# A feed-forward kernel on one Trainium2 core: down-weight blocks of 256 columns, and the sums of an up pair queued 12 ticks behind its request

## The chip, the cores and the metric

The kernel runs on one core of a Trainium2 chip. The metric is the device time of one execution in microseconds, as the median over runs. The engines are named as the profile names them: PE (TensorE, matmuls), DVE (VectorE), ACT (ScalarE), POOL (GpSimd) and SP (SyncE, which here issues the weight transfers). Each engine works through its own queue in the order in which the program wrote it.

## The reference, cut to what matters

The reference is one step of a two-layer hybrid backbone on 128 context tokens and 512 latent tokens, with a model width of 1024. Each layer ends in a gated feed-forward part, and the change lies in that part alone:

```
def conv_ffn(h, w_up, conv_w, conv_b, w_down):
    u = dwconv_centred(h @ w_up, conv_w, conv_b)
    val, g = jnp.split(u, 2, axis=-1)
    return (jax.nn.silu(g) * val) @ w_down
```

`w_up` is 1024 x 5632, `w_down` is 2816 x 1024, and the convolution has three taps along the tokens. The result, scaled by a gate, is added to the residual stream.

## The kernel before, in words

All products are made in float32 quality from float32r parts: a weight block is copied from HBM to a raw tile `wraw`, ACT rounds it to `whi` (L112), POOL subtracts to get `wlo` (L117), and each product takes three matmuls (`mm3`, L471 to L473). Tokens lie along the free axis: 644 columns (128 context, a gap of 4, 512 latent), taken in two halves of 322.

The 2816 hidden channels are 22 blocks of 128, in seven chunks of 3, 3, 3, 3, 3, 3 and 4 (`FF_CHUNKS`). The loop over chunks in `ffn` is

```
            for c, n in enumerate(FF_CHUNKS):
                ups(c, 0, early(c))
                if c:
                    down(c - 1)
                ups(c, early(c), n)
```

so that between two calls of `down` there are three up pairs. They are called A (the first after a down), B, and C (the one just ahead of the next down). An up pair (`up_pair`) makes value and gate of one hidden block from two up blocks of 128 columns by seven products of a Strassen-like scheme, in the order p1, p6, p5, p2, p7, p4, p3; each is 12 matmuls of 322 columns. Four of the seven use sums of the two weight blocks. `add_up` makes these on DVE (L139 to L142, tile `wsum`; L140 overwrites half of the second raw block in place), and `sum_part` splits them into `shi` (ACT) and `slo` (POOL for the first, DVE for the others, L119). Afterwards the pair's convolution (L1550 on ACT, then L317 on DVE, tile `ft`), the gate (L1566 on ACT, L1561 on DVE) and the split into `hidh` (ACT, L508) and `hidl` (DVE, L512) follow some ticks later.

`down` makes eight output tiles, 0 to 7; each is 18 matmuls (three hidden blocks, two halves, three terms) into one tile of PSUM named `wide`, which DVE adds to the residual `X` with two instructions (L317, 128x128 and 128x512). They are called X0 to X7. There are three `wide` buffers, used in turn by the down tiles and by the products (two products of a pair share one). So down tile n needs X(n-3) to be done; p1 and p6 of pair A need X5, p5 and p2 need X6, and p7 and p4 need X7.

The order of the work is written by a small planner. `tick` counts the program's position: one tick for three matmuls in a pair, two ticks for six matmuls in a down, so that a down tile has 6 ticks and a pair 28. `after(n, f)` writes f n ticks later. The class `Weights` holds the queue of weight blocks. `pump` requests the next block as long as a raw tile is free (`n_raw` = 3, used in turn); a raw tile comes free when its block has been split. `ahead` writes the splits of the next blocks, as far as there are free pairs of `whi`/`wlo` (`n_part` = 3, given back by `done`) and of `shi`/`slo` (`n_sum` = 4). For an up pair the order is add_up, split of the first block, two sums, split of the second block, the third sum. In `before` it writes `add_up` as soon as both blocks have been requested. `M.step` reads one block of the modulation maps with four matmuls and one DVE add; it runs beside the first feed-forward part until the maps are done, so the first four downs of layer 0 have it (their tiles are longer), and the last two of layer 0 and all six of layer 1 (called plain downs here) do not. The last chunk's down is another function (`last_down`) with blocks of 128 columns as before.

Of the kernel before, what the change touches and what calls it, by code (L numbers as in the profile page):

```python
# [9 lines left out]
F32 = mybir.dt.float32  # L10
# [11 lines left out]
NT = S0 + NS  # L22
NT2 = NT // 2
HALF = 322
OFF = 512 - HALF
# [8 lines left out]
HALVES = ((0, HALF), (HALF, NT))  # L34
# [5 lines left out]
FF_CHUNKS = (3, 3, 3, 3, 3, 3, 4)  # L40
# [2 lines left out]
N_STD = (2, 0, 3, 3)  # L43
N_WAIT = 1
AHEAD = 3
N_HID, N_FT = 4, 5
SUMS = (1, 8, 4)
FAST = (2, 2, 2, 2, 2, 1)
# [34 lines left out]
class Weights:  # L83
# [6 lines left out]
    def __init__(self, nc, pool, items):  # L90
        self.nc, self.pool, self.items = nc, pool, items
        self.loaded = self.freed = self.queued = self.next = 0
        self.raw, self.parts, self.pieces = {}, {}, []
        self.n_raw, self.n_part, self.n_sum = 3, 3, 4
        self.n_w = self.n_s = 0
        self.sums = self.over = None
        self.limit = len(items)

    def pump(self):
        while self.loaded < min(len(self.items), self.freed + self.n_raw, self.limit):  # L100
            ap, kt, w, _ = self.items[self.loaded]
            t = self.pool.tile([128, 8, 128], F32, name="wraw", tag="wraw", bufs=self.n_raw)[:, :kt, :w]
            self.nc.sync.dma_start(t, ap.rearrange("(k p) c -> p k c", p=128))
            self.raw[self.loaded] = t
            self.loaded += 1

    def split(self, pool, src, tag, bufs, low):
# [37 lines left out]
        self.parts.setdefault((i, "s"), []).append(  # L145
            self.split(self.sums, self.s[:, n], "s", self.n_sum, self.nc.vector if n else self.nc.gpsimd))

    def ahead(self, n=100):
        self.pump()
        for _ in range(n):  # L150
            if not self.pieces:
                i = self.queued
                if i == len(self.items):
                    return
                kind = self.items[i][3]
                if kind == "pair":
                    if not self.sums or self.loaded < i + 2:
                        return
                    self.pieces = [(0, lambda: self.add_up(i)), (1, lambda: self.block(i)),
                                   (2, lambda: self.sum_part(i, 0)), (2, lambda: self.sum_part(i, 1)),  # L160
                                   (1, lambda: self.block(i + 1)), (2, lambda: self.sum_part(i, 2))]
                    self.queued += 2
                else:
                    if self.loaded <= i or (kind == "held" and not self.over):
                        return
                    self.pieces = [(int(kind != "held"), lambda: self.block(i))]
                    self.queued += 1
            what, f = self.pieces[0]
            if (what == 1 and self.n_w == self.n_part) or (what == 2 and self.n_s == self.n_sum):
                return  # L170
            self.n_w += what == 1
            self.n_s += what == 2
            self.pieces.pop(0)
            f()
            self.pump()

    def upto(self, i):

        was = None
        while was != (self.queued, len(self.pieces)) and (self.queued <= i or self.pieces):  # L180
            was = self.queued, len(self.pieces)
            self.ahead(1)

    def get(self):
        for _ in range(8):
            if self.next not in self.parts:
                self.ahead(1)
        p = self.parts.pop(self.next)
        self.next += 1
        return p  # L190

    def get_pair(self):
        i = self.next
        while self.queued < i + 2 or (self.queued == i + 2 and self.pieces):
            self.ahead(1)
        return self.get(), self.get(), self.parts.pop((i, "s"))

    def done(self, w=1, s=0):
# [42 lines left out]
def tile_hybrid_step(ctx: ExitStack, tc: tile.TileContext, a, o):  # L241
# [121 lines left out]
    def add_w(ap, r0, kt, c0, w=128, kind=None):  # L363
        items.append((ap[r0:r0 + 128 * kt, c0:c0 + w], kt, w, kind))

    def held(n, n_std):
        return "held" if n >= n_std else None
# [32 lines left out]
    def ffn_items(l):  # L400
        up, dn = a["ffn_w_up"][l], a["ffn_w_down"][l]
        base = 0
        starts = []
        for n in FF_CHUNKS:
            starts.append(base)
            base += n

        def ups(c, j0, j1):
            for j in range(starts[c] + j0, starts[c] + j1):
                add_w(up, 0, 8, 128 * j, kind="pair" if j >= N_PLAIN else None)  # L410
                add_w(up, 0, 8, D_FF + 128 * j, kind="pair" if j >= N_PLAIN else None)

        def downs(c, last=False):
            for n in range(8):
                add_w(dn, 128 * starts[c], FF_CHUNKS[c], 128 * n, kind=held(n, N_STD[1 + 2 * l]) if last else None)
        for c, n in enumerate(FF_CHUNKS):
            ups(c, 0, early(c))
            if c:
                downs(c - 1)
            ups(c, early(c), n)  # L420
        downs(len(FF_CHUNKS) - 1, True)
        return starts
# [11 lines left out]


    k.bg, k.events, k.clock, k.count = [], [], 0, 0

    def after(n, f):
        heapq.heappush(k.events, (k.clock + n, k.count, f))
# [29 lines left out]
    def mm3(ps, w, x, c0, c1, p0, start, stop):  # L469
        (whi, wlo), (xhi, xlo) = w, x  # L470
        nc.tensor.matmul(ps[:whi.shape[-1], p0:p0 + c1 - c0], whi, xhi[:, c0:c1], start=start, stop=False)  # L471
        nc.tensor.matmul(ps[:whi.shape[-1], p0:p0 + c1 - c0], whi, xlo[:, c0:c1], start=False, stop=False)  # L472
        nc.tensor.matmul(ps[:whi.shape[-1], p0:p0 + c1 - c0], wlo, xhi[:, c0:c1], start=False, stop=stop)  # L473
# [6 lines left out]
    def wide():  # L480
        k.n_wide += 1
        return k.psum.tile([128, 1024], F32, name="wide", tag=k.wide_tag, bufs=k.wide_bufs)

    def gemm(xs, n=1, n_k=None, tail=True):

        n_k = n_k or len(xs)
        W.ahead()
        ws, ps = [], []
        for _ in range(n):
            ws.append(W.get())  # L490
            ps.append(wide())
        for kt, x in enumerate(xs):
            for w, p in zip(ws, ps):
                for c0, c1 in HALVES:
                    mm3(p, wk(w, kt), x, c0, c1, OFF + c0, kt == 0, kt == n_k - 1)
                tick(2)
        W.limit = len(items)
        W.done(n)
        M.step()
        if tail:  # L500
            W.ahead()
        return [p[:, OFF:OFF + NT] for p in ps]
# [995 lines left out]
    def ffn(l, final=None):  # L1498
        with ExitStack() as st:
# [124 lines left out]
            def down(c):  # L1624
                js = range(ffn_starts[c], ffn_starts[c] + FF_CHUNKS[c])
                until(lambda: all(j in hid for j in js))
                xs = [hid.pop(j) for j in js]
                for n in range(8):
                    ps = gemm(xs, 1, tail=False)[0]
                    for s, cols in STREAMS:  # L1630
                        fma(X[:, n, cols], ps[:, cols], modc[l][:, s, 40 + n:41 + n], X[:, n, cols])

# [349 lines left out]
```

## Time and profile before

| what | value |
|---|---|
| median of 3 runs | 2086.69 us (2076.94 to 2088.32) |
| profiled execution, its own time | 2080.74 us |
| its span on the core | 2078.7 us |
| mean granted TensorE clock | 0.962 of full speed |
| PE busy | 1880.9 us, 90% of the span |
| DVE busy | 1415.1 us, 68% |
| POOL busy | 1184.0 us, 57% |
| ACT busy | 964.7 us, 46% |

The profile is of a fourth execution, which took 2 us more than its span. Busy times are unions of instruction times on an engine; matmuls overlap each other at their ends, so PE can be busy without being at its peak. A row's releaser, shown as <-, is what ended the idle time before it.

### The profile page before, as it was taken

How to read it: one execution, taken by the hardware profiler on the slowest of the kernel's cores; microseconds unless marked ns; L12 is line 12 of the kernel's file. 1: busy time of each engine (PE TensorE's matmuls, PEld its weight loads, DVE VectorE, ACT ScalarE, POOL GpSimd, SP SyncE). 2: the span in 40 equal slices, each digit the busy share in tenths (PEclk: the TensorE clock that was granted, in tenths of full speed). 3: DMA queues.
4: the chain of work that ended last, by engine and by line, in shares of the span. 5: the costliest groups of instructions: out<-in, count | busy, mean ns of one | idle time of the engine just before them, and what ended most of it. 6: DMA issues, size and time to landing. Idle time of an engine off the chain costs nothing. (4 is left out here: it accounts for less than half of the span.)

```text
span 2078.7 us, 33613 instructions
## 1 busy us (share of the span) xinstructions
PE 1880.9 (90%) x12601; PEld 1719.6 (83%) x12601; DVE 1415.1 (68%) x2438; ACT 964.7 (46%) x1677; POOL 1184.0 (57%) x1528
## 2 busy tenths in 40 slices
PE   6878889999998999899999998988779899999997
PEld 4767668888887888798899997977679799999996
DVE  3477765655665337777778786676857778787874
ACT  3454453445444325433334344677725443443445
POOL 3235454333335445576557876478865577776772
PEclk9889999999999999999999999999889899999999
DMA  9554432112113342345542223112121122322221
GB/s 261 174 166 156 147 109 78 44 50 56 49 48 107 111 152 82 102 131 181 174 136 73 82 85 97 39 49 56 31 61 48 44 71 81 88 78 72 61 82 71
DMA packets 255577, 196.59 MB, mean 95 GB/s; under 512 B 13837, under 2 KB 233816, under 8 KB 255288
## 3 DMA queue, kind: packets, MB, share of 16 engines
q1 hardware_dynamic: 252664, 184.59, 29.6%
q0 software_dynamic: 2528, 7.13, 1.4%
q8 instruction: 99, 1.62, 0.3%
q10 hardware_dynamic: 224, 2.73, 0.3%
q14 instruction: 62, 0.51, 0.1%
HBM read 187.50 MB, written 6.92 MB: 94 GB/s over the span
## 5 line engine op out<-in xcount | busy, mean ns | idle before, releaser
L117 POOL TENSOR_TENSOR wlo<-wraw,whi 128x256 fp32r<-128x256 f32 (+1 forms) x835 | 710.7, 880 | 562.2 <-ACT whi L112 497.9
L471 PE MATMUL wide<-hhi,whi 128*128 128x322 f32 (+4 forms) x1072 | 358.7, 335 | 34.1 <-DVE X L317 15.2
L472 PE MATMUL wide<-hlo,whi 128*128 128x322 f32 (+4 forms) x1072 | 344.0, 321 | 7.5 <-DVE hlo L512 7.3
L473 PE MATMUL wide<-hhi,wlo 128*128 128x322 f32 (+4 forms) x1072 | 341.6, 319 | 0.0
L112 ACT CAST whi<-wraw 128x1024 fp32r<-128x1024 f32 (+1 forms) x259 | 217.4, 840 | 146.2 <-PE wide L473 71.1
L471 PEld LDWEIGHTS wide<-hhi,whi 128*128 128x128 f32 x1072 | 211.3, 197 | 52.9 <-ACT shi L112 15.4
L471 PE MATMUL gh<-hhi,whi 128*128 128x322 f32 (+3 forms) x688 | 232.1, 337 | 8.7 <-ACT zt L1178 8.7
L472 PEld LDWEIGHTS wide<-hlo,whi 128*128 128x128 f32 x1072 | 211.3, 197 | 12.2 <-DVE hlo L512 8.2
L472 PE MATMUL gh<-hlo,whi 128*128 128x322 f32 (+3 forms) x688 | 216.4, 315 | 1.3 <-DVE hlo L512 1.0
L473 PE MATMUL gh<-hhi,wlo 128*128 128x322 f32 (+3 forms) x688 | 215.9, 314 | 0.0
L473 PEld LDWEIGHTS wide<-hhi,wlo 128*128 128x128 f32 x1072 | 211.1, 197 | 0.0
L317 DVE SCALAR_TENSOR_TENSOR ft<-ft,PC 128x643 f32<-128x643 f32 x160 | 167.3, 1067 | 42.6 <-ACT ft L1550 40.6
L471 PE MATMUL wide<-hidh,whi 128*128 128x322 f32 (+2 forms) x600 | 191.3, 319 | 1.1 <-DVE ft L1608 1.1
L472 PE MATMUL wide<-hidl,whi 128*128 128x322 f32 (+2 forms) x600 | 187.0, 312 | 0.8 <-DVE hidl L512 0.8
L473 PE MATMUL wide<-hidh,wlo 128*128 128x322 f32 (+2 forms) x600 | 187.0, 312 | 0.0
L471 PEld LDWEIGHTS gh<-hhi,whi 128*128 128x128 f32 (+1 forms) x688 | 131.4, 191 | 33.7 <-issue 20.8
L317 DVE SCALAR_TENSOR_TENSOR X<-wide,modc,X 128x128 f32<-128x128 f32 (+3 forms) x276 | 128.0, 507 | 33.8 <-PE wide L473 33.8
L1550 ACT ACTIVATE ft<-ft,PC 128x644 f32<-128x644 f32 x80 | 73.9, 927 | 145.4 <-DVE ft L1615 135.3
L472 PEld LDWEIGHTS gh<-hlo,whi 128*128 128x128 f32 (+1 forms) x688 | 131.2, 191 | 2.4 <-DVE hlo L512 1.2
L473 PEld LDWEIGHTS gh<-hhi,wlo 128*128 128x128 f32 (+1 forms) x688 | 130.8, 190 | 0.6
L112 ACT CAST shi<-wsum 128x512 fp32r<-128x512 f32 x120 | 72.8, 617 | 123.8 <-DVE wsum L141 110.6
L471 PEld LDWEIGHTS wide<-hidh,whi 128*128 128x128 f32 x600 | 113.5, 189 | 14.5 <-issue 7.0
(379 smaller groups left out, 4606.6 us busy)
## 6 DMA issues: line engine op xcount, KB each, us to landing
wraw<-in_ffn_w_up_dram SPq DMA_DIRECT2D x88, 512.0 KB
mraw<-in_w_mod_dram SPq DMA_DIRECT2D x80, 512.0 KB
wraw<-in_ssd_attn_w_in_dram SPq DMA_DIRECT2D x42, 512.0 KB
wraw<-in_ffn_w_down_dram SPq DMA_DIRECT2D x96, 192.0 KB
E<-ad SPq DMA_DIRECT2D x16, 640.0 KB
mraw<-in_w_mod_dram SPq DMA_DIRECT2D x32, 256.0 KB
wraw<-in_ssd_attn_w_out_dram SPq DMA_DIRECT2D x16, 512.0 KB
wraw<-in_lru_w_in_dram SPq DMA_DIRECT2D x16, 512.0 KB
```

The costliest lines, as they stand in the source:

```text
L112: self.nc.scalar.copy(hi, src)
L117: low.tensor_sub(lo[:, q], src[:, q], hi[:, q].bitcast(F32))
L317: nc.vector.scalar_tensor_tensor(out, in0, scalar, in1, op0=op0, op1=op1, **kw)
L471: nc.tensor.matmul(ps[:whi.shape[-1], p0:p0 + c1 - c0], whi, xhi[:, c0:c1], start=start, stop=False)
L472: nc.tensor.matmul(ps[:whi.shape[-1], p0:p0 + c1 - c0], whi, xlo[:, c0:c1], start=False, stop=False)
L473: nc.tensor.matmul(ps[:whi.shape[-1], p0:p0 + c1 - c0], wlo, xhi[:, c0:c1], start=False, stop=stop)
L1550: after(at, lambda: nc.scalar.activation(out, u, AF.Identity, scale=par(cw, 2 * NF + t), bias=par(cb, t)))
```

## The change

A chunk's down weights are requested as four blocks of 256 columns in place of eight of 128 (384 KB each in place of 192 KB); `down` takes a block for two output tiles and gives it back after the second. The raw tile is the same 1024 columns, but laid out without gaps. The last chunk's down keeps its blocks. And `ahead` writes the sums of an up pair only when 12 ticks have passed since the request for its second block, unless the pair is needed at once (`get`, `get_pair` and `upto` pass `now=True`).

```
+LANDING = 12
...
     def pump(self):
         while self.loaded < min(len(self.items), self.freed + self.n_raw, self.limit):
             ap, kt, w, _ = self.items[self.loaded]
-            t = self.pool.tile([128, 8, 128], F32, name="wraw", tag="wraw", bufs=self.n_raw)[:, :kt, :w]
+            t = self.pool.tile([128, 1024], F32, name="wraw", tag="wraw", bufs=self.n_raw)[:, :kt * w].rearrange(
+                "p (k c) -> p k c", k=kt)
             self.nc.sync.dma_start(t, ap.rearrange("(k p) c -> p k c", p=128))
             self.raw[self.loaded] = t
+            self.asked[self.loaded] = self.clock()
...
-    def ahead(self, n=100):
+    def ahead(self, n=100, now=False):
...
                     if not self.sums or self.loaded < i + 2:
+                        return
+                    if not now and self.clock() < self.asked[i + 1] + LANDING:
                         return
...
         def downs(c, last=False):
+            if not last:
+                for n in range(4):
+                    add_w(dn, 128 * starts[c], FF_CHUNKS[c], 256 * n, 256)
+                return
             for n in range(8):
-                add_w(dn, 128 * starts[c], FF_CHUNKS[c], 128 * n, kind=held(n, N_STD[1 + 2 * l]) if last else None)
+                add_w(dn, 128 * starts[c], FF_CHUNKS[c], 128 * n, kind=held(n, N_STD[1 + 2 * l]))
...
                 for n in range(8):
-                    ps = gemm(xs, 1, tail=False)[0]
+                    W.ahead()
+                    if n % 2 == 0:
+                        whi, wlo = W.get()
+                    c = slice(128 * (n % 2), 128 * (n % 2) + 128)
+                    ps = wide()
+                    for kt, x in enumerate(xs):
+                        for c0, c1 in HALVES:
+                            mm3(ps, (whi[:, kt, c], wlo[:, kt, c]), x, c0, c1, OFF + c0, kt == 0, kt == len(xs) - 1)
+                        tick(2)
+                    W.done(n % 2)
+                    M.step()
+                    ps = ps[:, OFF:OFF + NT]
```

What this does to the queues is shown at three places of one plain down, the first of layer 1; the later ones have the same rows. On DVE, the rows around the sums of pair A before the change stand like this, beginning with X2 (two rows for each X):

```order
L317 SCALAR_TENSOR_TENSOR X<-wide,modc_113,X 128x128
L317 SCALAR_TENSOR_TENSOR X<-wide,modc_113,X 128x512
L1561 TENSOR_TENSOR ft<-ft 128x644
L512 TENSOR_TENSOR hidl<-ft,hidh 128x644
L317 SCALAR_TENSOR_TENSOR X<-wide,modc_113,X 128x128
L317 SCALAR_TENSOR_TENSOR X<-wide,modc_113,X 128x512
L317 SCALAR_TENSOR_TENSOR X<-wide,modc_113,X 128x128
L317 SCALAR_TENSOR_TENSOR X<-wide,modc_113,X 128x512
L139 TENSOR_TENSOR wsum<-wraw 128x512
L140 TENSOR_TENSOR wraw<-wraw 128x512
L141 TENSOR_TENSOR wsum<-wraw 128x512
L142 TENSOR_TENSOR wsum<-wraw,wsum 128x512
```

The same place on DVE after the change, beginning with X1 (lines are those of the changed kernel, where L143 to L146 are the sums, L1572 the gate's product, L523 `hidl`):

```order
L323 SCALAR_TENSOR_TENSOR X<-wide,modc_113,X 128x128
L323 SCALAR_TENSOR_TENSOR X<-wide,modc_113,X 128x512
L143 TENSOR_TENSOR wsum<-wraw 128x512
L144 TENSOR_TENSOR wraw<-wraw 128x512
L145 TENSOR_TENSOR wsum<-wraw 128x512
L146 TENSOR_TENSOR wsum<-wraw,wsum 128x512
L323 SCALAR_TENSOR_TENSOR X<-wide,modc_113,X 128x128
L323 SCALAR_TENSOR_TENSOR X<-wide,modc_113,X 128x512
L1572 TENSOR_TENSOR ft<-ft 128x644
L523 TENSOR_TENSOR hidl<-ft,hidh 128x644
L323 SCALAR_TENSOR_TENSOR X<-wide,modc_113,X 128x128
L323 SCALAR_TENSOR_TENSOR X<-wide,modc_113,X 128x512
```

The sums of pair A moved from behind X4 to behind X1, and with that ahead of X2, of the gate's product of pair C and of its `hidl`.

Further on in DVE's queue come the sums of pair B. Before the change the rows are these, from X6 on:

```order
L317 SCALAR_TENSOR_TENSOR X<-wide,modc_113,X 128x128
L317 SCALAR_TENSOR_TENSOR X<-wide,modc_113,X 128x512
L119 TENSOR_TENSOR slo<-wsum,shi 128x512
L139 TENSOR_TENSOR wsum<-wraw 128x512
L140 TENSOR_TENSOR wraw<-wraw 128x512
L141 TENSOR_TENSOR wsum<-wraw 128x512
L142 TENSOR_TENSOR wsum<-wraw,wsum 128x512
L317 SCALAR_TENSOR_TENSOR X<-wide,modc_113,X 128x128
L317 SCALAR_TENSOR_TENSOR X<-wide,modc_113,X 128x512
L119 TENSOR_TENSOR slo<-wsum,shi 128x512
L1603 TENSOR_TENSOR ft<-wide,ft 128x322
```

After the change they are these, from X5 on:

```order
L323 SCALAR_TENSOR_TENSOR X<-wide,modc_113,X 128x128
L323 SCALAR_TENSOR_TENSOR X<-wide,modc_113,X 128x512
L123 TENSOR_TENSOR slo<-wsum,shi 128x512
L143 TENSOR_TENSOR wsum<-wraw 128x512
L144 TENSOR_TENSOR wraw<-wraw 128x512
L145 TENSOR_TENSOR wsum<-wraw 128x512
L146 TENSOR_TENSOR wsum<-wraw,wsum 128x512
L323 SCALAR_TENSOR_TENSOR X<-wide,modc_113,X 128x128
L323 SCALAR_TENSOR_TENSOR X<-wide,modc_113,X 128x512
L323 SCALAR_TENSOR_TENSOR X<-wide,modc_113,X 128x128
L323 SCALAR_TENSOR_TENSOR X<-wide,modc_113,X 128x512
```

The sums of pair B stood between X6 and X7; now they stand ahead of both.

On ACT, the casts from the middle of the down to the first block of pair A (128x1024) stand like this before the change (`hidh` is L508, the gate's activation L1566):

```order
L112 CAST whi<-wraw 128x384 x2
L1566 ACTIVATE ft<-ft 128x644
L112 CAST whi<-wraw 128x384
L508 CAST hidh<-ft 128x644
L112 CAST whi<-wraw 128x384 x2
L112 CAST whi<-wraw 128x1024
L112 CAST shi<-wsum 128x512 x2
```

After the change they stand like this:

```order
L116 CAST whi<-wraw 128x768
L1577 ACTIVATE ft<-ft 128x644
L519 CAST hidh<-ft 128x644
L116 CAST whi<-wraw 128x1024
L116 CAST shi<-wsum 128x512 x2
L116 CAST whi<-wraw 128x1024
```

The down casts became fewer and larger, and the cast of pair A's first block moved up to stand right behind `hidh`; POOL's queue follows the same order with its `wlo` pieces.

## Rows read from the trace of the kernel before

**Rows 1.** The page: busy time, share of the span and instructions by engine.
```profile
PE 1880.9 (90%) x12601; PEld 1719.6 (83%) x12601; DVE 1415.1 (68%) x2438; ACT 964.7 (46%) x1677; POOL 1184.0 (57%) x1528
```

**Rows 2.** Windows: stretch, length, busy us (instructions) by engine, granted clock, DMA.
```profile
1733.00:1796.00 63.00, 60.86 (x399) 60.43 (x398) 49.79 (x68) 26.14 (x41) 45.99 (x55) 0.97 0.26 76
1796.00:1859.00 63.00, 59.67 (x399) 58.97 (x397) 50.20 (x68) 26.04 (x41) 46.39 (x55) 1.00 0.26 76
...
1922.00:1984.00 62.00, 60.25 (x394) 60.05 (x395) 49.26 (x67) 26.15 (x41) 46.41 (x55) 0.97 0.27 77
```

**Rows 3.** Waits of PE, 1640 to 2020: us in total, times, longest.
```profile
PE wide L471 <- DVE X L317: 13.9, 9, 2.1
```

**Rows 4.** Waits of PE, 860 to 1150, the downs with map steps.
```profile
PE wide L471 <- DVE X L317: 1.6, 3, 0.8
```

**Rows 5.** Waits of PE, 1150 to 1250, the plain downs of layer 0.
```profile
PE wide L471 <- DVE X L317: 5.0, 3, 2.1
```

**Rows 6.** Timeline of PE at three places: start, us, operation, [idle before <-releaser].
```profile
1735.60 0.39 PE L471 MATMUL wide<-hhi,whi 128*128 128x322 f32 x1 [2.14 <-DVE X L317]
1735.82 0.31 PE L472 MATMUL wide<-hlo,whi 128*128 128x322 f32 x1
1735.97 0.31 PE L473 MATMUL wide<-hhi,wlo 128*128 128x322 f32 x1
...
1798.51 0.39 PE L471 MATMUL wide<-hhi,whi 128*128 128x322 f32 x1 [2.15 <-DVE X L317]
...
1806.91 0.39 PE L471 MATMUL wide<-t3h,shi 128*128 128x322 f32 x1 [1.03 <-DVE X L317]
```

**Rows 7.** Timeline of DVE, one plain down and the start of pair A.
```profile
1717.13 3.72 DVE L317 SCALAR_TENSOR_TENSOR ft<-ft,PC 128x643 f32<-128x643 f32 x3
1720.77 1.91 DVE L317 SCALAR_TENSOR_TENSOR X<-wide,modc,X 128x128 f32<-128x128 f32 x4
...
1724.44 0.83 DVE L512 TENSOR_TENSOR hidl<-ft,hidh 128x644 fp32r<-128x644 f32 x1 [0.80 <-ACT hidh L508]
1725.19 1.92 DVE L317 SCALAR_TENSOR_TENSOR X<-wide,modc,X 128x128 f32<-128x128 f32 x4
1730.80 1.12 DVE L139 TENSOR_TENSOR wsum<-wraw 128x512 f32<-128x512 f32 x1 [3.69 <-DMA wraw<-in_ffn_w_up_dram]
...
1733.84 0.69 DVE L142 TENSOR_TENSOR wsum<-wraw,wsum 128x512 f32<-128x512 f32 x1
1734.45 1.00 DVE L317 SCALAR_TENSOR_TENSOR X<-wide,modc,X 128x128 f32<-128x128 f32 x2
...
1738.83 0.69 DVE L139 TENSOR_TENSOR wsum<-wraw 128x512 f32<-128x512 f32 x1 [0.50 <-DMA wraw<-in_ffn_w_up_dram]
...
1741.84 1.11 DVE L142 TENSOR_TENSOR wsum<-wraw,wsum 128x512 f32<-128x512 f32 x1
1742.88 1.00 DVE L317 SCALAR_TENSOR_TENSOR X<-wide,modc,X 128x128 f32<-128x128 f32 x2
```

**Rows 8.** Timeline of ACT, same stretch.
```profile
1710.03 0.51 ACT L112 CAST whi<-wraw 128x384 fp32r<-128x384 f32 x1
...
1723.68 0.73 ACT L508 CAST hidh<-ft 128x644 fp32r<-128x644 f32 x1 [1.59 <-DVE ft L1561]
...
1728.13 1.05 ACT L112 CAST whi<-wraw 128x1024 fp32r<-128x1024 f32 x1 [2.17 <-PE wide L473]
```

**Rows 9.** Timeline of POOL, same stretch; a 384-column block takes two pieces.
```profile
1713.72 1.16 POOL L117 TENSOR_TENSOR wlo<-wraw,whi 128x256 fp32r<-128x256 f32 x2
1714.85 0.76 POOL L1614 TENSOR_TENSOR ft<-ft,x 128x322 f32<-128x322 f32 x1
...
1729.26 3.27 POOL L117 TENSOR_TENSOR wlo<-wraw,whi 128x256 fp32r<-128x256 f32 x4 [1.85 <-ACT whi L112]
```

**Rows 10.** Timeline of SP's queue: requests for the second blocks of pairs A and B.
```profile
1726.32 0.37 SPq L103 DMA_DIRECT2D wraw<-in_ffn_w_up_dram  x1
...
1734.68 0.37 SPq L103 DMA_DIRECT2D wraw<-in_ffn_w_up_dram  x1
```

More of the change, by code (lines that the diff above doesn't have):

```diff
@@ L97, in __init__ @@
         self.limit = len(items)
+        self.clock, self.asked = (lambda: 0), {}
     def pump(self):
@@ L181, in upto @@
             was = self.queued, len(self.pieces)
-            self.ahead(1)
+            self.ahead(1, True)
     def get(self):
@@ L186, in get @@
             if self.next not in self.parts:
-                self.ahead(1)
+                self.ahead(1, True)
         p = self.parts.pop(self.next)
@@ L194, in get_pair @@
         while self.queued < i + 2 or (self.queued == i + 2 and self.pieces):
-            self.ahead(1)
+            self.ahead(1, True)
         return self.get(), self.get(), self.parts.pop((i, "s"))
@@ L436, in tile_hybrid_step @@
     k.bg, k.events, k.clock, k.count = [], [], 0, 0
+    W.clock = lambda: k.clock
     def after(n, f):
```

## The prediction

> **What bounds the kernel now.** I read the page first: PE is busy for 90% of the span, and no other engine is above 68% [rows 1]. Then the windows of one period (three pairs and a plain down) of layer 1: PE is busy 60 to 61 of 63 us, while DVE comes to 50 of 63 [rows 2]. So in the part that the change touches PE is the bound, and all that can be won is its idle time and its half-clock time; but DVE is near enough to full that a few microseconds of waiting in its queue reach PE.
>
> The waits of PE give the amount. Between 1640 and 2020 PE waits 13.9 us in nine waits for DVE's X [rows 3]; in the two plain downs of layer 0 it is 5.0 us in three [rows 5]; in the downs with map steps only 1.6 us [rows 4]. Together that is 20.5 us. The clock adds to it: in two of the three windows shown the granted clock is 0.97, a loss of some 0.03 x 63 = 1.9 us each [rows 2].
>
> The timelines say why. At 1735.60 the first matmul of pair A has waited 2.14 us for X, at 1798.51 another 2.15 us; there, at 1806.91, p7 (the operand t3h) waits 1.03 us more [rows 6]. DVE had X3 and X4 done by 1727.1 and then stood idle 3.69 us in the sums of pair A, whose second block was still in flight. The sums took 1730.80 to 1734.5, X5 came only after them, and PE went on [rows 7]. The request for that block is at 1726.32, so it took 4.5 us to the first sum [rows 10, 7]. The sums of pair B stand ahead of X7 in the same way: they begin at 1738.83 and X7 at 1742.88 [rows 7].
>
> **A clock for one down.** Matmuls start 0.15 us apart (1735.82, 1735.97 [rows 6]). A tile of 18 takes 2.7 us, a product of 12 takes 1.8. The eight tiles end at 1735.60 - 2.14 = 1733.5, so tile 0 starts at 1711.9 and tile n ends at 1711.9 + 2.7(n+1). With no wait p5 would start at 1733.5 + 3.6 = 1737.1 and p7 at 1740.7. Before, p7 starts 1806.91 - 1798.51 + 2.15 = 10.55 us after the end of tile 7, which is 1744.0 on this clock. In the period shown the half clock ate the second wait instead, and p7 starts at about 1735.6 + 7.2 + 1.6 = 1744.4. I take 1744.2 for before, a loss of 3.5 us per plain down.
>
> **The change, part by part.** *Fewer, larger blocks.* ACT casts 384 columns in 0.51 and 1024 in 1.05 [rows 8], so 768 is about 0.83: four of those are 3.3 us per down, where eight small ones were 4.1. POOL takes 1.16 us for a block's two pieces and 3.27 for four full ones [rows 9]: three full ones are 2.45, four blocks 9.8 us, where eight were 9.3. SP issues four requests for eight. None of this is on PE's path by its sum, since ACT and POOL are idle 37 and 17 us of such a window [rows 2]. But the first blocks sit in POOL's queue ahead of pair C's last additions: the block of 1713.72 stands just ahead of L1614 [rows 9], and its split grows by 1.3 us. What is late next is C's convolution on ACT and DVE. Of the conv rows on DVE (three in 3.72 us from 1717.13 [rows 7]) the last two wait for it. X1, done at 1721.7 before, comes at 1721.7 to 1722.3.
>
> *An earlier request for pair A.* Three blocks of the down are split by the time tile 0 starts, so A's second block is asked for when that POOL split ends: 1713.72 + 2.45 plus up to 0.8 of delay, about 1716.2 to 1717. With 4.5 us it lands by 1721.5. The idle 3.69 us of DVE is gone: this part does what it says.
>
> *But the sums now stand behind X1.* They start at 1721.7 to 1722.3 and take 3.1 us (POOL idle) to 3.7 (as from 1730.80 to 1734.5 [rows 7]). X2 ends 0.93 later, at 1725.7 to 1726.9, while tile 5 is due at 1725.4: PE waits 0.4 to 1.5 us. X3 comes after the gate's product and `hidl`, some 3.2 us after X2, against a tile 6 then due 2.7 later: another 0.5 to 0.8.
>
> *The sums of pair B are the new place.* They need B's second block, which goes into the raw tile of A's first block and so waits for POOL's split of that. The chain, from X2 on: the gate's product 0.83, `hidh` on ACT 0.73, A's first cast right behind it 1.05, four POOL pieces 3.27 [rows 8, 9], then the request. From X2's end at 1725.7 that makes 1731.8, and with a later X2 and slower pieces 1733. A request takes 1738.83 - 1734.68 = 4.15 us to the first sum [rows 10, 7], so the sums of B start at 1735.9 to 1737.1. They take 3.7 to 4.1 (POOL is at work then), and X6, which stands behind them now, ends 0.95 later: 1740.6 to 1742. p5 was due at 1737.1 plus the 1 to 2 us just lost. It starts at 1740.8 to 1742; p7, 3.6 later, at 1744.4 to 1745.6, and X7 is then long done. Against 1744.2 before, that is +0.2 to +1.4 us per plain down. I take +0.8, the middle, because the two ends differ only by whether DVE and POOL get in each other's way, and both kinds of rows stand in this stretch. So the 12 ticks do not cover it: they are two tiles, 5.4 us, from the writing of A's first split, but that split runs far behind its place in the program.
>
> At one place a page speaks against the change. The last of the four sums takes 0.69 us at 1733.84 and 1.11 at 1741.84, where POOL is at work [rows 7]; I priced the sums of B between these. The Trainium skill (SBUF — State Buffer, Who interferes with whom) says that a DVE instruction with two SBUF inputs and a GpSimd instruction that reads SBUF block each other fully, not in part. By that rule four sums could each wait out a POOL piece.
>
> **The sum.** Eight plain downs (six in layer 1, two in layer 0) x 0.8 = +6.4 us, bounds +1.6 to +11.2. The four downs with map steps have tiles longer by four matmuls and a DVE add; there the chain has about 5 us more room before p5, so I count their 1.6 us as won, bounds 0 to -1.6. The half clock: before, one that follows the first wait is hidden by the second; after, one that follows the wait of p5 is not, and costs its 1.6 us; one that follows the wait of tile 5 is. I take it in one down out of six or so, +2 us, bounds 0 and 8 x 1.6 = +13. Together +6.4 - 1.6 + 2 = +7 us. The profiled execution took 2080.74 us, which makes about 2088; it is 6 us below the median of the runs shown, and from that median, 2086.7, I come to 2094.
>
> **The rivals.** *The stall vanishes (faster).* If B's second block lands before DVE reaches the sums of B, X6 follows at once. DVE is there after X5 and one `slo`, at about 1734; p5 stays unstalled if X6 is done by about 1738.5, so the sums must start by 1733.8, 2.1 us earlier than my best chain. It needs A's first cast to run about 2 us earlier, as if it didn't sit behind `hidh`. Then a plain down loses only the 1 to 2 us at tiles 5 and 6: a gain of 8 x 2 + 1.6 = 18 us, or 2069. For it: DVE's 3.69 us of idle do go. Against it: the rows on ACT and POOL in the order of the change.
>
> *The change does nothing in sum.* The losses of tiles 5, 6 and p5 just replace those of p1 and p7: 2087 with a few us either way. It is the low end of my chain.
>
> *The clock falls at every new wait.* The wait of p5 is 2 to 3 us, as long as the ones of 2.14 to 2.15 of which some are followed by a half clock. If all are: 6.4 + 13 - 1.6 = +18, 2105.
>
> *DVE is blocked a whole POOL piece per sum.* A piece is 3.27 / 4 = 0.82, so each sum would take up to 0.69 + 0.82 = 1.51 and the four of B 6.0 in place of 4: 8 x 2 = +16 more, about 2110. The row of 1.11 speaks against it, and it is the rule of the Trainium skill (SBUF — State Buffer) at its strictest.
>
> **How the numbers follow.** My forecast has 0.5; the stall vanishing 0.17; nothing in sum 0.15; the clock 0.13; the blocked sums 0.05. A measurement of this kernel tells about 0.5%, 10 us, from no change. The first rival is faster by that. Forecast cases up to +10 us are the same, and I put 0.3 of its 0.5 there, with 0.14 from nothing in sum and 0.02 from a weak form of the clock; the rest, 0.37, is slower. The range goes from 2078 (below "nothing in sum" and short of a full gain) to 2108 (the clock case), and leaves out most of the first rival and the blocked sums.
>
> **What would show it.** Right: on DVE no long wait for a DMA ahead of pair A's sums; waits of PE for X at tiles 5 and 6 (on `hidh`) of 0.4 to 1.5 us, none at p1, and one of 2 to 4 us at p5 (operand `hhi`, block `whi`); the request for B's second block at 1731.8 to 1733 on this clock, with DVE waiting for it. Wrong: p5 without a wait and PE's waits for X in 1640 to 2020 well under 14 us; or new waits in the pairs, from late `slo`, which I priced at nothing because those sums are written earlier than before.

## The result: 1.6% slower

The changed kernel takes 2116.38 us (median of 4 runs, 2113.11 to 2117.38) where the kernel before takes 2086.02 (also of 4): a ratio on record of 1.0161, 95% interval [1.0138, 1.0185]. The plain quotient of the two medians is 1.0146 and lies in that interval. The prediction had 2094 us and a range up to 2108. So the direction was the one forecast, and the size was about four times the forecast +7 us. To a slowdown clear of the noise it had given 0.37, less than to no change.

The page of the changed kernel gives the busy times. PE is busy 14 us longer than in [rows 1], the span is 32.4 us longer (2078.7 to 2111.1), and the mean granted clock is 0.959 in place of 0.962.

```profile
span 2111.1 us, 33257 instructions
...
PE 1895.1 (90%) x12601; PEld 1726.4 (82%) x12601; DVE 1410.7 (67%) x2438; ACT 955.1 (45%) x1629; POOL 1154.4 (55%) x1480
```

Where the 32.4 us are can be read from marks that both timelines have: in each feed-forward part the one matmul of the first pair that waits 3.9 to 4.1 us for DVE (`hhi,shi`), and the first matmul of its `last_down`. In layer 0 they stand at 848.88 and 1267.28 before and at 847.23 and 1286.97 after: 418.4 us have become 439.7. In layer 1 they stand at 1633.51 and 2026.86, and at 1652.62 and 2060.80: 393.4 have become 408.2. That is +21.3 and +14.8; all the rest of the kernel together is 3.8 us shorter.

### The profile page after: what moved, and what is told of

The parts are those of the page before. It is cut to its first block, busy times and chain, and to the rows that moved or that the text cites. A ratio compares the mean times of both kernels' runs of the same rounds, so it can differ in the third digit from the quotient of the medians.

```text
span 2111.1 us, 33257 instructions
## 1 busy us (share of the span) xinstructions
PE 1895.1 (90%) x12601; PEld 1726.4 (82%) x12601; DVE 1410.7 (67%) x2438; ACT 955.1 (45%) x1629; POOL 1154.4 (55%) x1480
## 5 line engine op out<-in xcount | busy, mean ns | idle before, releaser
L121 POOL TENSOR_TENSOR wlo<-wraw,whi 128x256 fp32r<-128x256 f32 x787 | 672.3, 884 | 653.2 <-ACT whi L116 572.3
L116 ACT CAST whi<-wraw 128x1024 fp32r<-128x1024 f32 (+2 forms) x211 | 208.4, 989 | 151.8 <-PE wide L484 74.4
L323 DVE SCALAR_TENSOR_TENSOR ft<-ft,PC 128x643 f32<-128x643 f32 x160 | 175.2, 1109 | 46.8 <-ACT ft L1561 44.8
L483 PEld LDWEIGHTS wide<-hidl,whi 128*128 128x128 f32 x600 | 115.4, 192 | 1.0 <-DVE hidl L523 1.0
```

Of the source, the lines that this page charges most:

```text
L116: self.nc.scalar.copy(hi, src)
L121: low.tensor_sub(lo[:, q], src[:, q], hi[:, q].bitcast(F32))
L323: nc.vector.scalar_tensor_tensor(out, in0, scalar, in1, op0=op0, op1=op1, **kw)
```

## The profile after

**A plain down.** This is DVE's timeline of one, in layer 1 (start, duration, instruction, in brackets the idle time ahead of it and what ended it), from X1 to X6 and X7; it answers to [rows 7].

```profile
1740.48 1.00 DVE L323 SCALAR_TENSOR_TENSOR X<-wide,modc,X 128x128 f32<-128x128 f32 x2
1741.40 0.99 DVE L143 TENSOR_TENSOR wsum<-wraw 128x512 f32<-128x512 f32 x1
...
1743.88 0.69 DVE L146 TENSOR_TENSOR wsum<-wraw,wsum 128x512 f32<-128x512 f32 x1
1744.49 1.00 DVE L323 SCALAR_TENSOR_TENSOR X<-wide,modc,X 128x128 f32<-128x128 f32 x2
...
1755.52 0.99 DVE L143 TENSOR_TENSOR wsum<-wraw 128x512 f32<-128x512 f32 x1 [2.93 <-DMA wraw<-in_ffn_w_up_dram]
...
1758.84 1.10 DVE L146 TENSOR_TENSOR wsum<-wraw,wsum 128x512 f32<-128x512 f32 x1
1759.87 1.91 DVE L323 SCALAR_TENSOR_TENSOR X<-wide,modc,X 128x128 f32<-128x128 f32 x4
```

The sums of A start right behind X1, with no wait for a transfer; X2 stands behind them. The sums of B wait 2.93 us for their second block, and X6 stands behind those. On SP's queue these are the requests for the second blocks of A and B. The one of B came 5.9 us after X2's end (1745.49), and the sums 4.15 us after it.

```profile
1736.00 0.37 SPq L106 DMA_DIRECT2D wraw<-in_ffn_w_up_dram  x1
...
1751.37 0.37 SPq L106 DMA_DIRECT2D wraw<-in_ffn_w_up_dram  x1
```

On PE's timeline of the same down the first row here is the start of tile 0; then come the rows with a wait for X: the first matmuls of tiles 5 and 6 and of p5, and, further down, of p5 behind the next down. Behind the first p5 the matmuls of 0.31 us become ones of 0.47, for 3.2 us. The granted clock of that stretch (1762.6 to 1765.8) is 0.50, the lower of its two levels (1.2 in place of 2.4 GHz); this is what half clock means here, and nothing hides it at this place.

```profile
1730.59 0.41 PE L482 MATMUL wide<-hidh,whi 128*128 128x322 f32 x1
...
1745.63 0.39 PE L482 MATMUL wide<-hidh,whi 128*128 128x322 f32 x1 [1.10 <-DVE X L323]
...
1748.92 0.39 PE L482 MATMUL wide<-hidh,whi 128*128 128x322 f32 x1 [0.39 <-DVE X L323]
...
1761.01 0.39 PE L482 MATMUL wide<-hhi,whi 128*128 128x322 f32 x1 [2.93 <-DVE X L323]
...
1762.59 0.47 PE L483 MATMUL wide<-hlo,whi 128*128 128x322 f32 x1
...
1827.39 0.61 PE L482 MATMUL wide<-hhi,whi 128*128 128x322 f32 x1 [2.93 <-DVE X L323]
```

The down of 1745.63 and the four behind it (1812.01, 1878.39, 1943.26, 2007.41) are 66.4, 66.4, 64.9 and 64.2 us apart, 65.4 in the mean. Before, p1 of 1672.83 and of 1986.43 are five periods apart, 62.7 us each. The windows of two of the periods show the clock that separates those of 66.4 us from those of 64.2 and 64.9: 0.97 and 1.00 (columns as in [rows 2]).

```profile
1761.00:1827.00 66.00, 61.69 (x396) 60.32 (x396) 48.91 (x67) 25.39 (x37) 43.78 (x52) 0.97 0.24 72
...
1894.00:1958.00 64.00, 59.95 (x397) 58.63 (x396) 48.45 (x67) 25.40 (x37) 43.30 (x50) 1.00 0.25 75
```

**A down with map steps.** The waits of PE between 860 and 1150 are no longer those of [rows 4]. None is for X; `M.step` waits for its map block, 9.8 us in four times, and twice for DVE, 2.3 us.

```profile
PE mt L338 <- DMA mraw<-in_w_mod_dram: 9.8, 4, 3.7
PE mt L338 <- DVE wsum L143: 2.3, 2, 1.6
```

The longest of them is the second of these rows of PE, and the next fence has SP's queue ahead of it. Between the map request of 926.92 and that of 938.58 stand the two requests of an up pair, and both have to wait until a raw tile is free. The block that PE waits for at 944.77 is the one of 938.58. There are two map tiles in turn, and PE had read the one that this block goes into by 934.74 (the row of 934.10). So the request came 3.8 us late, and PE's wait is 3.7.

```profile
934.10 0.64 PE L338 MATMUL mt<-mraw,scp 128*32 128x256 f32 x8
...
944.77 1.08 PE L338 MATMUL mt<-mraw,scp 128*32 128x256 f32 x8 [3.71 <-DMA mraw<-in_w_mod_dram]
```

```profile
926.92 0.44 SPq L229 DMA_DIRECT2D mraw<-in_w_mod_dram  x1
935.34 3.15 SPq L106 DMA_DIRECT2D wraw<-in_ffn_w_up_dram  x2
938.58 7.65 SPq L229 DMA_DIRECT2D mraw<-in_w_mod_dram  x3
```

In the kernel before, SP's queue in the same stretch has a map request behind each small down block or two.

```profile
926.55 0.45 SPq L223 DMA_DIRECT2D mraw<-in_w_mod_dram  x1
933.01 3.41 SPq L103 DMA_DIRECT2D wraw<-in_ffn_w_down_dram  x2
936.51 2.20 SPq L223 DMA_DIRECT2D mraw<-in_w_mod_dram  x2
939.46 0.38 SPq L103 DMA_DIRECT2D wraw<-in_ffn_w_down_dram  x1
942.10 0.33 SPq L223 DMA_DIRECT2D mraw<-in_w_mod_dram  x1
943.29 0.38 SPq L103 DMA_DIRECT2D wraw<-in_ffn_w_down_dram  x1
945.56 0.33 SPq L223 DMA_DIRECT2D mraw<-in_w_mod_dram  x1
```

So the theory after the result has two separate parts. In the plain downs X6 stands behind sums of B whose block is in flight. In the downs with map steps the map requests stand on SP's queue behind requests that wait for a raw tile. Its rivals: the larger blocks are slow in themselves (POOL, DMA engines, raw tiles); or a wait removed anywhere comes back elsewhere.

The gate, the second half of the change, does nothing here. With blocks of 256 columns a gate of 0 ticks and one of 12 give the same program, instruction for instruction and wait for wait, on all five engines: the splits of the down blocks already hold the sums back to the same ticks. Whatever the changed kernel loses is the blocks' doing, with the order that they bring.

## The experiments

The kernel before ran beside each on the same chip (medians of 2078 to 2081 us there), so ratios to it are compared. "Map waits" are PE's waits for `mraw` in 860 to 1150; "layer 0" and "layer 1" are the lengths between the marks above. These three columns are in us and come from the one profiled execution of each kernel, the ratio from all of its executions.

| kernel | ratio to before, 95% | layer 0 | layer 1 | map waits |
|---|---|---|---|---|
| before | 1 | 418.4 | 393.4 | 0 |
| after | 1.0161 [1.0138, 1.0185] | 439.7 | 408.2 | 9.8 |
| e3_maps_on_act | 1.0099 [1.0080, 1.0118] | 424.3 | 406.5 | 0.7 |
| e5_plain_only | 1.0113 [1.0096, 1.0131] | 428.1 | 404.9 | 0 |
| e4_landing24 | 1.0096 [1.0073, 1.0119] | 440.4 | 391.5 | 14.5 |
| e13_landing13 | 1.0004 [0.9988, 1.0019] | 430.5 | 385.4 | 11.3 |
| e7_both_undone | 0.9978 [0.9965, 0.9991] | 423.0 | 391.3 | 4.3 |

### The maps, in two ways

e3_maps_on_act asks for the map blocks from ACT's queue during the first feed-forward part:

```
-            self.nc.sync.dma_start(t, ap)
+            self.queue.dma_start(t, ap)
...
+    M.queue = nc.scalar
     ffn(0)
```

> The changed kernel, but during the first feed-forward part the blocks of the modulation maps are requested from ACT's queue and no longer from SP's. Theory (in the downs with map steps the map requests stand on SP's queue behind both requests of an up pair, the second of which waits for a raw tile): the waits of PE for mraw and for the DVE add of the map block (9.8 and 2.3 us in 860 to 1150) and their half clock go, 12 to 16 us: 2100 to 2104 us, ratio 1.006 to 1.009; layer 1 stays as in the changed kernel (20.7 us of waits for X). Rival (larger blocks take the DMA engines or raw tiles from the maps, whatever queue asks for them): the waits for mraw stay, 2113 to 2117 us, ratio 1.013 to 1.016.

e5_plain_only keeps blocks of 128 columns in the four downs that have map steps:

```
+NARROW = 4
...
-            if not last:
+            if not last and (l or c >= NARROW):
```

> The changed kernel, but the first four downs of layer 0, those with map steps, keep eight blocks of 128 columns. Theory (the loss has two separate parts): layer 0's waits for mraw go, and the plain downs keep their waits at tile 5, 6 and p5, so about 16 us less than the changed kernel, 2098 to 2104 us, ratio 1.005 to 1.009; this sizes the two parts. Rival (the loss of layer 0 comes from the gate in the plan and not from the blocks): the time stays at 2112 to 2117 us.

Both are faster than the changed kernel, where the rivals had next to no gain, but both gained less than forecast: the ratios are 0.001 and 0.002 above the theory's ranges. Layer 0 gets 15.4 us back by the one and 11.7 by the other. In layer 1, where neither edit changes anything, it is 1.7 and 3.3, so by some 3 us such a length differs between executions. In e3 the blocks are as large as in the changed kernel, and yet the map waits are gone: it was the place in SP's queue, not the transfers. The Trainium skill (DMA: Bandwidth & Descriptors, Rules for kernel authors) says that spreading DMAs over the issuing engines brings no bandwidth and only saves issue time. Here it brings 0.6%, because a request no longer stands behind one that waits.

The control for it is the same edit on the kernel before, in which PE waited for 1.3 us in all ahead of a map step.

> The kernel before with one edit, the maps requested from ACT's queue during the first feed-forward part. Theory (only the changed order of requests on SP made the maps late; in the kernel before they wait 1.4 us at most in SP's queue and cost PE 1.3 us): no difference, ratio 0.997 to 1.002. Rival (the other queue is worth something by itself, and the gain of e3_maps_on_act and e8_wide_a12_maps is partly that): ratio 0.995 or less.

e12_before_maps has the ratio 1.0033 [1.0021, 1.0045], a little slower than expected: PE's waits for X in 860 to 1150 go from 1.6 [rows 4] to 6.4 us. So the other queue is worth nothing by itself. ACT's waits and its timeline show what it costs:

```profile
ACT whi L112 <- PE mt L333: 70.6, 30, 5.2
```

```profile
1029.67 0.34 ACTq L224 DMA_DIRECT2D mraw<-in_w_mod_dram  x1
1030.13 1.05 ACT L112 CAST whi<-wraw 128x1024 fp32r<-128x1024 f32 x1 [2.94 <-PE mt L333]
```

Now the casts of the weight blocks stand on ACT's queue behind map requests, and these wait until PE has read a map tile. Before, no cast waits for `mt`. In the third of the four downs the request for B's second block comes 26.6 us after the down's first matmul, where it came after 25.7, and PE waits 2.2 us for X at p7 in place of 0.3. A request that waits holds up what stands behind it here too, only on another queue. The links between the cast and X were not followed one by one.

### The place of the sums, with blocks of 256 columns

e4_landing24 changes one number, `LANDING = 24`: A's sums go behind X3, B's behind X7, C's behind the last combination of pair A.

> The changed kernel with a gate of 24 ticks in place of 12. In the program pair A's sums then stand behind X3 and pair B's behind X7. Theory (in plain downs the order of the sums against the X is what costs, not the size of the blocks): PE's waits at tiles 5 and 6 and at p5 go in all eight plain downs, and with them the waits of before at p1; the map waits of layer 0 stay. 2078 to 2086 us, ratio 0.995 to 1.000. Rival (the larger blocks themselves make casts and POOL pieces late, or later sums make shi and slo late in the pairs): waits for shi or slo of 2 us or more per down take their place, 2105 us or more, ratio 1.009 or more.

It had the ratio 1.0096, which by its number alone is the rival's. The traces say otherwise: layer 1 takes 391.5 us in place of 408.2, less than before, with no wait of the sums for a transfer, and all that is lost is in layer 0, where the map waits have grown to 14.5 us. The theory's range was missed by two things: those 4.7 us more, and a wait of 2.0 us per plain down that is left at tile 7, for the X4 that stands behind the sums of A.

e13_landing13 is the closest cut: `LANDING = 13`. In all twelve downs one tick more moves the sums of B from ahead of X6 to behind it (in those with map steps also behind the map block's add), and that is all: the queues of the other four engines are the same, instruction for instruction.

> The changed kernel with a gate of 13 ticks in place of 12, one number. In the program only the sums of pair B move in the plain downs, from ahead of X6 to behind it; those of A stay behind X1, and C's ahead of pair A's last combination. Theory (the wait of 2.9 us at p5 is X6 behind sums of B whose block is in flight): that wait goes in all eight plain downs, some 23 us of waits and a few of half clock, the waits at tiles 5 and 6 and layer 0's for mraw stay: ratio to the kernel before 1.000 to 1.006. Rival (the wait only moves on: p7 waits for X7, or the combinations wait behind C's sums, as with blocks of 128 columns, where three orders all kept about 3 us per period): ratio 1.010 or more.

This settles the plain downs. The ratio falls from 1.0161 to 1.0004, and layer 1 takes 385.4 us, 22.8 less. That is 8 less than before the change, so the larger blocks are not slow in themselves. The waits of PE between 1640 and 2020 were 20.7 us for X in the changed kernel; in e13_landing13 they are the first of these rows (the other has one wait of 3.9 at the part's start):

```profile
PE wide L482 <- DVE X L323: 7.4, 10, 1.1
PE wide L482 <- DVE ft L1614: 5.3, 7, 3.9
```

On DVE the block of B is still late, but now X6 is ahead of it, and X7, behind it, is in time for p7. PE keeps only its waits at tiles 5 and 6, of 1.09 and 0.37 us, and no stretch at half clock follows a wait in a plain down any more. The wait on DVE was never the cost; what stood behind it was. (The releaser named in the second row is a POOL piece of `wlo`, which the sums do not read; the piece of `slo` that they do wait for ended at 1746.31, so the block in flight came last.)

```profile
1745.63 1.00 DVE L323 SCALAR_TENSOR_TENSOR X<-wide,modc,X 128x128 f32<-128x128 f32 x2
1749.18 1.15 DVE L143 TENSOR_TENSOR wsum<-wraw 128x512 f32<-128x512 f32 x1 [2.55 <-POOL wlo L121]
...
1752.66 1.12 DVE L146 TENSOR_TENSOR wsum<-wraw,wsum 128x512 f32<-128x512 f32 x1
1753.70 1.00 DVE L323 SCALAR_TENSOR_TENSOR X<-wide,modc,X 128x128 f32<-128x128 f32 x2
```

### The gate alone, with blocks of 128 columns

e2_landing_only keeps eight blocks per down and has only the gate, which is not idle there: A's sums go behind X5, B's behind X7.

```
-            if not last:
-                for n in range(4):
-                    add_w(dn, 128 * starts[c], FF_CHUNKS[c], 256 * n, 256)
-                return
```

> Blocks of 128 columns as before, and only the gate of 12 ticks. In the program pair A's sums then stand behind X5 and pair B's behind X7, where before they stood behind X4 and between X6 and X7. Theory (what PE waits for is an X queued behind sums whose block is still in flight): the nine waits for X in 1640 to 2020 (13.9 us) and the three in 1150 to 1250 (5.0 us) go, about 19 us and one or two microseconds of half clock, so 2064 to 2070 us, ratio 0.990 to 0.993. The windows of layer 0 with map steps stay as before. Rival: sums that start that late make shi and slo late for p6 and p5, and PE waits there for as long as it did at p1: 2082 to 2092 us, ratio 0.998 to 1.003.

The ratio is 1.0044 [1.0027, 1.0061], above the theory's range and the rival's: the theory's gain did not come. The waits for X are gone as expected, but PE's waits in 1640 to 2020 are now these, six times some 3 us behind a combination of pair A (L1620), and not where the rival had put them:

```profile
PE wide L478 <- DVE ft L1620: 18.1, 6, 3.2
PE wide L478 <- DVE ft L1610: 1.0, 3, 0.3
```

DVE shows the same picture one pair further on. The sums of C wait, and the combination stands behind them. Their block was requested at 1687.48, 3.95 us earlier (the releaser named is again a piece of `wlo`; the piece of `slo` that the sums wait for ended at 1689.30, so the block in flight came last).

```profile
1691.43 1.19 DVE L143 TENSOR_TENSOR wsum<-wraw 128x512 f32<-128x512 f32 x1 [2.32 <-POOL wlo L121]
...
1695.15 0.48 DVE L1620 TENSOR_TENSOR ft<-wide,ft 128x322 f32<-128x322 f32 x1
```

Two more runs moved the sums apart, with a gate for each pair of a chunk (A, B, C): (12, 12, 28) in e6_small_late_c, (12, 0, 28) in e9_small_b_between.

```
-                    if not now and self.clock() < self.asked[i + 1] + LANDING:
+                    if not now and self.clock() < self.asked[i + 1] + LANDING[self.place(i)]:
...
+    def place(self, i):
+        if self.items[i - 1][3] != "pair":
+            return 0
+        return 2 if self.items[i + 2][3] != "pair" else 1
```

> Blocks of 128 columns and the gate of 12 ticks for pairs A and B as in e2_landing_only, but 28 ticks for pair C, which puts the sums of C behind the last combination of pair A (L1622 there) and leaves the rest of the order. Theory (the wait of 2.8 to 3.2 us per plain down in e2_landing_only is the combination L1620 of pair A standing behind sums of C whose block is in flight): these eight waits go, 24 us and their half clocks, and none comes back, since C starts more than 10 us later: ratio to the kernel before 0.989 to 0.994. Rival (the period is set by the round of the raw tiles: split, request, 4 us, sums, and PE's wait only shows where it closes): a wait of 2 to 3 us per period turns up at another place, ratio 0.999 to 1.005.

> As e6_small_late_c, but the sums of B between X6 and X7 as in the kernel before. Theory: X7 stands behind them again, and PE waits up to 1 us at p7 in each plain down, so 4 to 8 us more than e6_small_late_c, ratio 0.993 to 0.997. Rival (what counts is how early the sums of B free their raw tiles): waits in the pairs get shorter than in e6_small_late_c, and the time is the same or 3 to 6 us less.

Neither gained, as the rivals had it: 1.0065 [1.0044, 1.0085], beyond the rival's range too, and 1.0051 [1.0033, 1.0070], which is not clearly less. PE's waits in 1640 to 2020, of e6 and then of e9:

```profile
PE wide L483 <- DVE ft L1615: 15.7, 5, 3.4
PE wide L483 <- DVE ft L1620: 1.2, 1, 1.2
```

```profile
PE wide L483 <- DVE X L328: 17.9, 6, 3.1
PE wide L483 <- DVE ft L1615: 0.9, 2, 0.4
```

With small blocks four orders (before, e2, e6, e9) lose about 3 us per plain down: at p1 and p7, behind C's sums, behind C's sums and pair A's convolution, or at p7 alone. What they share is a late request for A's second block: before, 14.4 us after the start of tile 0 (1711.9 on the prediction's clock, 1726.32 in [rows 10]), and 12.8 to 14.5 us after it in the downs of the other three. With 256 columns it came 5.4 us after it (1730.59 and 1736.00 above), 9 us earlier. So the large blocks do have their use, which the changed kernel spends on its order. That this request is the cause of the 3 us is argued from these rows; no run took it apart, and that no order without the loss exists with small blocks is not shown.

### Both undone, and a version that beats both kernels

e7_both_undone is e4_landing24 with the maps on ACT's queue.

> The changed kernel with the gate of 24 ticks (e4_landing24) and the maps requested from ACT's queue (e3_maps_on_act). Theory (the two losses are separate): layer 1's feed-forward part as in e4_landing24 (391 to 392 us), layer 0's 418 to 421 us, no waits for mraw: ratio 0.997 to 1.002. Rival (they share a cause, such as late POOL pieces): less than the sum is won back, ratio 1.005 or more.

The ratio of 0.9978 [0.9965, 0.9991] is inside the theory's range, and the lengths add up: 15.4 us of layer 0 (e3) and 16.7 of layer 1 (e4) by themselves, 16.7 and 16.9 together. So the two losses are separate. Layer 0 comes to 423.0, 2 us above the theory: 4.3 us of map waits stay.

e8_wide_a12_maps has gates (12, 14, 30) and the maps on ACT's queue; e10_order_only is the same with the maps on SP's; e11_a18 is e8 with (18, 14, 30).

> Blocks of 256 columns and maps on ACT's queue, with the sums of pair A behind X1 as in the changed kernel, but those of B between X6 and X7 (14 ticks) and those of C behind pair A's combinations (30 ticks). Theory (in the changed kernel the wait at p5 is X6 behind sums of B whose block is in flight): of 4.7 us per plain down only the 1.1 and 0.4 at tiles 5 and 6 stay, X7 is in time for p7, and layer 1's part comes to 386 to 390 us: ratio 0.993 to 0.998. Rival (B's block lands later still, since its request hangs on ACT and POOL and not on the place of the sums, and stalls p7 or pair B for as long): ratio 1.002 or more.

> e8_wide_a12_maps with the maps requested from SP again: the changed kernel with nothing but other places for the sums of B and C. Theory (order and map queue are separate): layer 1's part as in e8_wide_a12_maps, layer 0's waits for mraw back: ratio 0.994 to 0.999. Rival (the queue of the maps did the larger part in e8_wide_a12_maps): ratio 1.005 or more.

> e8_wide_a12_maps with the sums of pair A 18 ticks behind the request, which puts them behind X2, ahead of the gate's product and hidl of pair C. Theory (the 0.9 and 0.4 us at tiles 5 and 6 are X2 and X3 behind the sums of A): the wait at tile 5 goes, X3 comes about as tile 6 needs it, 4 to 9 us less than e8_wide_a12_maps: ratio 0.984 to 0.987. Rival (X3 is late by what X2 no longer is, since sums, product and hidl now all stand ahead of it): no gain, ratio 0.988 to 0.992.

e8 takes 2058.66 us, 0.9882 [0.9861, 0.9904], better than expected. A period is 61.4 us long (tile 5 of 1714.37 and of 1775.75), PE's waits in it are 0.88, 0.36 and 0.64, and the clock is full:

```profile
1714.40:1775.80 61.40, 59.52 (x397) 58.82 (x397) 48.00 (x68) 25.40 (x37) 43.27 (x51) 1.00 0.27 78
```

e10 has 0.9954 [0.9937, 0.9971], as expected: the maps' queue is worth 0.7% here, and 0.6% in e3. Against e13, which it differs from in the place of C's sums, it gains 0.5%. Of that the rows show only that the first pair of each part waits 2.0 us where it waited 3.9 to 4.3; where the rest comes from is open.

e11 has 0.9872 [0.9856, 0.9889], which is not distinguishable from e8. The wait at tile 5 went, as the theory said, and one of 1.13 to 1.15 at tile 6 took its place, as the rival said: the two waits of 1.24 us became one of 1.15.

## Why the prediction was wrong, step by step

**The step that failed** is "The four downs with map steps ... so I count their 1.6 us as won, bounds 0 to -1.6". The X waits there did go. But I costed those downs by X alone and didn't follow SP's queue, where the map requests now stand behind both requests of an up pair. That costs layer 0 between 11.7 us (e5) and 15.4 us (e3), a term with the other sign and seven to ten times the size. The lengths agree: a period of layer 0's plain downs is 66.4 us (1165.69 to 1232.08) in place of 62.6 (1161.50 to 1224.08), which leaves, as an estimate, 21.3 - 2 x 3.8 = 13.7 us to the other four. None of my rivals had this place, and none of my signs looked at it: nearly all signs of being right came, and the time was wrong.

**The plain downs: right mechanism, undersized term.** Every row that the prediction named is there: no wait for a transfer ahead of A's sums, waits at tile 5 (1.1 us, forecast 0.4 to 1.5), at tile 6 (0.39, forecast 0.5 to 0.8), none at p1, and one at p5 of 2.9 (forecast 2 to 4) on `hhi,whi`. The chain behind it holds too, at the late end of each bound or just past it: the second block of B was requested 5.9 us after X2's end, where I had 6.1 (its four terms add up to 5.9), and its sums took 4.35 us (1755.52 to 1759.87), where I had 3.7 to 4.1. On the prediction's clock (tile 0 at 1711.9, 18.7 us earlier) X1 ends at 1722.8, forecast 1721.7 to 1722.3; A's request stands at 1717.3, forecast 1716.2 to 1717; B's at 1732.7, forecast 1731.8 to 1733; and p5 at 1742.3, forecast 1740.8 to 1742. Each plain down was to cost 0.8, bounds 0.2 to 1.4. It cost 1.4 and 2.2 in the two periods at almost full clock (64.15 and 64.87 against 62.72), at the upper bound and above it, and 2.7 in the mean. Layer 1 is 14.8 us longer; the forecast has 6 x 0.8 and its part of the half clock, some 6.

**The half clock, undersized too.** It was taken "in one down out of six or so", +2 us. It follows the wait at p5 in five of the eight plain downs (at 1181.07, 1247.46, 1761.01, 1827.39 and 2022.79), for 11 or 12 matmuls, the last time for 21. At 0.27 us from start to start in place of 0.15 that makes, as an estimate, 8 us, within the bounds of 0 and 13. The direction of the argument was right: the wait at p5 has nothing behind it that hides a slow stretch.

**The rivals.** The stall did not vanish, because the sums of B stood ahead of X6; with one tick more it did (e13), but with the map loss the time was still only that of before. "The clock falls at every new wait" gave a near number, 2105, by luck: the clock fell at five of the eight, and the larger share came from elsewhere. "DVE is blocked a whole POOL piece per sum" came nearest with 2110, by luck too: a whole piece was not seen. The last three sums of B, with POOL at work without a break from 1753.15 to 1760.53, took 1.10 to 1.12 us and POOL's pieces beside them 1.17 to 1.19; the last three of A, with POOL idle, took 0.69, and a piece by itself takes 0.73. The Trainium skill (SBUF — State Buffer, Who interferes with whom) has the two engines block each other fully. The trace bears out an interference and not this strictest reading: a sum takes 0.42 us more, not a whole piece more.

## What to carry to other kernels

A change of block size also changes which requests stand behind which: follow every queue that a moved request passes, above all for loads that have nothing to do with the change, since a request that waits for a buffer holds up all behind it. Work that waits for a transfer costs nothing by its wait, but by what stands behind it in its engine's queue; so look for the one instruction that a slower engine needs next, and put it ahead. The same holds on a queue that issues transfers and computes too: a request moved there to free one queue can hold up the work of the other (e12). A gate in steps of the program is no gate in time: find out whether it moves anything at all, and try the neighbouring values, of which here one step was worth 1.6%.

## What was not expected of the hardware

The same transfers, asked for from another engine's queue, gave 0.6 to 0.7% back with the large blocks (e3 against after, e8 against e10), and cost 0.3% in the kernel before (e12). A block took 4.15 us from request to use in the plain down shown, as long as before [rows 10, 7], though down blocks of twice the size share the queue. DVE's sums and POOL's pieces, running side by side, both took some 60% longer (0.69 to 1.11 and 0.73 to 1.18 us), so neither engine waited out the other's whole instruction.
